# Adaptive-norm columns summed by VectorE alone, from weights laid out by output column

## The chip, the core and the metric

One core of a Trainium2 chip runs the program. Time is device microseconds of one execution, the median of three runs. TensorE (PE in the profile) multiplies, VectorE (DVE), ScalarE (ACT) and GpSimd (POOL) work on whole tiles, and SyncE (SP) issues the transfers (DMA).

## The reference, cut to what matters

One layer of a hybrid encoder on 1024 tokens of width 1024: an attention branch that selects 256 keys for each query, a state-space (SSD) branch, a merge, and a SwiGLU feed-forward part. Everything is float32. The part that the change touches is the modulation at the top, one vector of six times 1024 numbers:

```python
mod = (jax.nn.silu(c) @ ada_w + ada_b)[:, None, :]
shift_m, scale_m, gate_m, shift_f, scale_f, gate_f = jnp.split(mod, 6, axis=-1)
h = rmsnorm(x, pre_norm_mix) * (1.0 + scale_m) + shift_m
...                                            # both branches work on h
x = x + gate_m * rmsnorm(mix, post_norm_mix)
h2 = rmsnorm(x, pre_norm_ffn) * (1.0 + scale_f) + shift_f
```

and the state-space branch's time steps:

```python
dt = jax.nn.softplus((dt_raw + dt_bias).astype(jnp.float32))
dA = (dt * A).reshape(...);  a_cum = jnp.cumsum(dA, axis=-1)
decay = jnp.exp(a_cum[..., -1:] - a_cum);  chunk_decay = jnp.exp(a_cum[..., -1])
```

## The kernel before, in words

Activations lie transposed: 128 channels on the partitions, tokens along the row in two halves of 512. A product in float32 is three matmuls of rounded parts (high by high, high by low, low by high). Weights of the large products come through `Stream` (`wraw`, then `whi` by ScalarE at L158 and `wlo` by GpSimd or VectorE at L159), two pieces of 4 x 128 x 128 ahead of PE.

`mod` has 48 columns of 128 channels. The first 16 (shift and scale of the mixer) are made by PE right at the start (`ada_mm`, `ada_end`). The other 32 aren't needed before the merge, late in the program, and are made by `ada_slow`, one column j at a time: two halves of the weights (`adaw`, 128 input channels on the partitions, 4 x 128 output channels in the row, 256 KB each) are loaded into two buffers, GpSimd multiplies each by silu(c) (`cs`, L329) and adds the two (L330), VectorE sums the remaining four pieces (L331, into `adas`), and `ada_col` sums over the partitions with one matmul against a column of ones (L297, `adap`, two records in the profile) and adds the bias on VectorE (L298, into `mod`).

These columns are issued in the attention stage. `attention` goes through 32 steps: 8 head pairs `hp`, four blocks of 256 queries `u` each, in the order 0, 2, 1, 3 (`U_ORDER`). A step makes the queries (`puq`, then `qh` on ScalarE and `ql` on VectorE at L821), the logits of two tiles of 128 queries and two heads (`plg`, L847), adds bias or mask and takes the running extreme on VectorE (L856, `lg` and `mx`), takes exponentials on ScalarE, and in the same step transposes the probabilities of the step before (`pt`, copied to `pc` by VectorE or ScalarE) and multiplies them with the values (`po`, L896). Blocks u = 2 and 3 have two `plg` banks to each tile and head and twelve `mx` pieces; u = 0 has four. Convolution work of the state-space branch is woven in (`fill`: `pw` on PE at L244, `cv` on VectorE at L1073, L1075 and L1090). PSUM places come from two rings: `bank`, five deep (`puq`, `plg`, `po`, `adap`, every other `pt`), and `bank_d`, three deep. At a step's end `beside()` calls `ada_next`, which starts column j and finishes the one started three steps before:

```python
    def ada_next():
        next(sums, None)
        j = next(slow, None)
        if late and (j is None or len(late) > 2):
            ada_col(*late.pop(0))
        if j is not None:
            late.append(ada_slow(j))
```

Ahead of attention stand the input projections (`FILL`: five groups of convolutions, 16 tiles of z, 8 of a gate), and beside them the indexer, whose `rel` pieces VectorE weights with `widx` and sums into `acc` (L654), and the search for the 256th largest score (`Ranked`). The state-space branch's `dt`, `acum`, `decay` and `cdec` are made in `dt_part` before the indexer and are used after attention, in `ssd_in` and `ssd_out`.

What sets the order: a scheduler places each engine's instructions by a simulated clock when the program is built, under the data's own dependences and those added by hand. In attention PE runs in the order written (`in_order`), the other engines don't. Every engine and SP's queue of transfers works through its own list in order and waits at its head.

Of the kernel before, what the change touches and what calls it, by code (L numbers as in the profile page):

```python
# [69 lines left out]
def build(tc, a, dbg=None, stop=99, slots=None):  # L70
# [223 lines left out]

    def ada_col(j, acc):
        p = bank("adap")
        T.matmul(p[:, 0:1], acc, onec, start=True, stop=True)  # L297
        V.tensor_tensor(mod[:, j:j + 1], p[:, 0:1], col("ada_b", j), op=OP.add)  # L298

    cs32 = sm.tile([P, 8, 32], F32, name="cs32", tag="r2", bufs=1)  # L300
# [14 lines left out]
    def ada_end(k, acc):  # L315
# [4 lines left out]
        V.scalar_tensor_tensor(amul[:, k:k + 1], mod[:, 8 + k:9 + k], 1.0, col("pre_mix", k), op0=OP.add, op1=OP.mult)  # L320

    def ada_slow(j):

        acc = sm.tile([P, P], F32, name="adas", bufs=4)
        ts = [wp.tile([P, 4, P], F32, name="adaw", tag="adaw", bufs=2) for h in range(2)]
        for h, t in enumerate(ts):
            tc.add_manual_dep(SP.dma_start(t, a["ada_w"][j - 16][:, 4 * h:4 * h + 4]).ins, ada_after[0], mybir.DependencyInfo(
                mybir.DependencyClass.NoSync, mybir.DependencyReason.DATA), reason="behind")
            behind(G.tensor_tensor(t, t, cs[:, 4 * h:4 * h + 4, None].to_broadcast([P, 4, P]), op=OP.mult))  # L329
        G.tensor_tensor(ts[0], ts[0], ts[1], op=OP.add)  # L330
        V.tensor_reduce(acc, ts[0].rearrange("p k m -> p m k"), axis=AX.X, op=OP.add)  # L331
        return j, acc

# [203 lines left out]

    widx = con.tile([P, NT, 16], F32, name="widx")
    dt = con.tile([P, NT, 32], F32, name="dt")
    tmp = [R("dt_tmp", (P, 4, NT, 32)) for _ in range(2)]  # L540
# [10 lines left out]
    def dt_part():  # L551
# [23 lines left out]
        T.matmul(ptot[:, 0:128], ones, dAv[:, :, 1, :], start=False, stop=True)  # L575
        acum = con.tile([P, NT, 32], F32, name="acum")
# [3 lines left out]
        decay = con.tile([P, NT, 32], F32, name="decay")  # L580
# [3 lines left out]
        cdec = con.tile([P, NCH, 32], F32, name="cdec")  # L584
        S.activation(cdec, tot, AF.Exp)
# [10 lines left out]
        dump("acum", acum)  # L596
        return acum, decay, cdec

    acum, decay, cdec = dt_part()


# [327 lines left out]
    def attention(steps, beside, fill, nf):  # L929

        ahead = biases(*steps[0])
        for n, s_ in enumerate(steps + [None]):
            nxt = iter(())
            if s_ is not None:
                hp, u = s_
                if u == U_ORDER[0]:
                    vt = vp.tile([P, NT, P], F32, name="vt", bufs=1)
                    SP.dma_start(vt, d_v[hp])
                    att["w"] = small_weights(a["w_uq"][hp]), vt
                uq, vt = att["w"]  # L940
                PR = {}
                nms, ahead = ahead, biases(*steps[n + 1]) if n + 1 < len(steps) else None
                nxt = att_scores(u, uq, nms, PR)
            prev = att.get("prev")
            out, turns = (att_out(*prev), 2 * prev[1] + 2) if prev else (iter(()), 0)
            order = [nxt]
            for i in range(4):
                order += [out] * (-(-(i + 1) * turns // 4) - order.count(out)) + [nxt]
            order.append(out)
            k = 0  # L950
            for i, g in enumerate(order):
                next(g, None)
                while k < nf[n] and k * len(order) < nf[n] * (i + 1):
                    next(fill, None)
                    k += 1
            if s_ is not None:
                att["prev"] = (hp, u, vt, PR)
            beside()

    slow, late = iter(range(16, 48)), []  # L960

    def ada_next():

        next(sums, None)
        j = next(slow, None)
        if late and (j is None or len(late) > 2):
            ada_col(*late.pop(0))
        if j is not None:
            late.append(ada_slow(j))

# [168 lines left out]
    V.tensor_scalar(halved, halved, 0.5, None, op0=OP.mult)  # L1139
# [1021 lines left out]
def arrays_of(inp):  # L2161
# [53 lines left out]
```

## Time and profile before

| | |
|---|---|
| median of 3 runs | 2335.45 us (2332.7 to 2337.65) |
| the profiled execution | 2334.56 us, span 2332.5 us |
| PE busy | 2298.1 us, 99% |
| VectorE, ScalarE, GpSimd busy | 71%, 52%, 42% |
| granted clock of TensorE | 0.996 |
| attention | from 675 to 1116 us of the span |
| the 32 columns (L327 to L331) | transfers from 405 us on, last reduction at 1092 us |
| their `adap` matmuls | 719 to 1116 us |

A row of a group of instructions reads: line, engine, operation, what is written from what, shapes, count | busy us, mean ns of one | idle us of the engine before them and what ended it. A row of a window reads: from and to, length, then the busy time (and the count) of PE, PE's weight loads, VectorE, ScalarE and GpSimd, the clock granted, the share of the DMA engines and GB/s.

### The profile page before, as it was taken

Reading aid. Unit: us, or ns where it says so; the run is one execution under the profiler, and the core shown is the slowest. Engines: PE = TensorE matmul, PEld = TensorE weight load, DVE = VectorE, ACT = ScalarE, POOL = GpSimd, SP = SyncE. Lnnn points to the kernel's source line nnn. Section 1 sums busy time; section 2 is a strip of 40 time slices with the busy share of each in tenths; the row PEclk is TensorE's granted clock in tenths of the full one; section 3 lists DMA queues with packets and bytes.
Section 4 is the critical chain, followed back from the end, with each engine's and each line's share of the span. In section 5 each row is a group of like instructions: output and inputs, shape, how many; then the busy total and the mean of one; then the engine's idle time right before and its main releaser. Section 6 shows DMA issues by size and latency. Waiting matters only on the chain. (4 is left out here: it accounts for less than half of the span.)

```text
span 2332.5 us, 35045 instructions
## 1 busy us (share of the span) xinstructions
PE 2298.1 (99%) x11736; PEld 1886.0 (81%) x11736; DVE 1646.2 (71%) x3185; ACT 1220.1 (52%) x2354; POOL 985.3 (42%) x787
## 2 busy tenths in 40 slices
PE   8999999999999999999999999999999999999997
PEld 5878888888888888888888888878788888888886
DVE  5466887599676777677667879675778776646685
ACT  4346666467635555555767766434555222235542
POOL 1435552522244656564345443100122554444556
PEclk9999999999999999999999999999999999999998
DMA  7137542622233444344689999674573454438664
GB/s 274 64 126 246 190 172 93 200 96 95 100 111 123 130 129 141 128 132 142 210 254 291 296 275 326 223 229 144 182 244 125 154 162 155 145 116 274 202 201 155
DMA packets 251715, 411.26 MB, mean 176 GB/s; under 512 B 25568, under 2 KB 93328, under 8 KB 251536
## 3 DMA queue, kind: packets, MB, share of 16 engines
q1 hardware_dynamic: 238288, 387.48, 50.5%
q10 hardware_dynamic: 13248, 21.56, 3.1%
q8 instruction: 92, 1.51, 0.3%
q14 instruction: 87, 0.71, 0.1%
HBM read 304.84 MB, written 107.24 MB: 177 GB/s over the span
## 5 line engine op out<-in xcount | busy, mean ns | idle before, releaser
L159 POOL TENSOR_TENSOR wlo<-wraw,whi 128x512 fp32r<-128x512 f32 x152 | 208.2, 1370 | 305.5 <-ACT whi L158 277.8
L1774 PE MATMUL p<-xh,wr 128*128 128x512 f32 x880 | 271.8, 389 | 0.0
L158 ACT ACTIVATE whi<-wraw 128x512 fp32r<-128x512 f32 x238 | 149.1, 628 | 207.9 <-issue 58.7
L1774 PEld LDWEIGHTS p<-xh,wr 128*128 128x128 f32 x880 | 165.2, 188 | 34.3
L1768 POOL TENSOR_TENSOR wr<-a,wr 128x512 fp32r<-128x512 f32 x82 | 114.7, 1407 | 133.8 <-ACT wr L1767 104.1
L1774 PE MATMUL p<-xl,wr 128*128 128x512 f32 x440 | 171.2, 389 | 0.0
L255 POOL TENSOR_TENSOR fwl<-fw,fwh 128x512 fp32r<-128x512 f32 (+1 forms) x78 | 107.0, 1384 | 105.1 <-ACT fwh L254 59.6
L273 POOL TENSOR_TENSOR r<-v,nhalf 128x4 f32<-128x4 f32 (+1 forms) x17 | 25.5, 1499 | 255.4 <-DVE v L271 255.4
L1767 ACT ACTIVATE wr<-a 128x512 fp32r<-128x512 f32 x107 | 66.6, 629 | 126.2 <-PE p L1774 88.2
L859 ACT ACTIVATE lg<-lg,mx 128x256 f32<-128x256 f32 (+7 forms) x128 | 99.1, 774 | 57.8 <-DVE mx L856 57.3
L654 DVE SCALAR_TENSOR_TENSOR acc<-rel,widx,acc 128x384 f32<-128x384 f32 (+2 forms) x90 | 102.1, 1157 | 16.2 <-ACT rel L649 16.1
L329 POOL TENSOR_TENSOR adaw<-adaw,cs 128x512 f32<-128x512 f32 x64 | 68.1, 1065 | 102.5 <-DMA adaw<-ada_w 85.0
L1774 PE MATMUL p<-h2h,wr 128*128 128x512 f32 x352 | 110.0, 390 | 0.0
L704 ACT ACTIVATE junk<-acc,cand__2216 128x1024 bf16<-128x1024 f32 (+2 forms) x96 | 86.3, 898 | 39.5 <-DVE cand__2216 L747 30.7
L649 ACT ACTIVATE rel<-prel 128x512 f32<-128x512 f32 (+3 forms) x160 | 76.9, 523 | 47.1 <-PE prel L648 46.3
L1774 PEld LDWEIGHTS p<-xl,wr 128*128 128x128 f32 x440 | 82.6, 188 | 17.2
L1698 PE MATMUL pos<-yh,wlo 128*128 128x512 f32 x224 | 87.9, 392 | 2.2 <-DVE wlo L159 2.1
L702 DVE TENSOR_SCALAR_CACHE_REDUCE junk<-acc,cand__2225 128x896 bf16<-128x896 f32 (+2 forms) x96 | 88.5, 922 | 1.5
L856 DVE CUSTOM_DVE_ANT_0 lg<-plg,nm 128x256 f32<-128x256 f32 (+1 forms) x128 | 51.5, 403 | 52.7 <-PE plg L847 52.0
L1768 POOL TENSOR_TENSOR wr<-s,wr 128x512 fp32r<-128x512 f32 x40 | 55.0, 1375 | 78.4 <-ACT wr L1767 70.8
L1698 PE MATMUL pos<-yh,whi 128*128 128x512 f32 x224 | 87.8, 392 | 0.0
L1698 PE MATMUL pos<-yw,whi 128*128 128x512 f32 x224 | 87.3, 390 | 0.0
(692 smaller groups left out, 7415.4 us busy)
## 6 DMA issues: line engine op xcount, KB each, us to landing
wraw<-w_in SPq DMA_DIRECT2D x129, 256.0 KB, 2.9
a<-w_ffn_in SPq DMA_DIRECT2D x122, 256.0 KB, 3.4
al<-d_a SPq DMA_DIRECT2D x88, 256.0 KB, 4.5
yl<-d_y SPq DMA_DIRECT2D x72, 256.0 KB, 4.9
adaw<-ada_w SPq DMA_DIRECT2D x64, 256.0 KB, 3.2
al<-d_ac SPq DMA_DIRECT2D x32, 512.0 KB, 5.6
d_a<-g SPq DMA_DIRECT2D x42, 256.0 KB, 2.4
ada<-ada_p SPq DMA_DIRECT2D x16, 512.0 KB, 7.9
```

What stands on the lines that cost most here:

```text
L158: self.hi = behind(S.activation(hi[:, :kt], raw[:, :kt], AF.Copy))
L159: self.lo = behind(self.eng[len(self.tiles) % len(self.eng)].tensor_tensor(lo[:, :kt], raw[:, :kt], f(hi[:, :kt]), op=OP.subtract))
L255: (lo_eng or V).tensor_tensor(lo, src, f(hi), op=OP.subtract)
L329: behind(G.tensor_tensor(t, t, cs[:, 4 * h:4 * h + 4, None].to_broadcast([P, 4, P]), op=OP.mult))
L649: S.activation(rel[:, 512 * b:512 * b + w_], pr[:, 0:w_], AF.Relu)
L654: V.scalar_tensor_tensor(acc[i][:, 0:n], rel[:, 0:n], ws, acc[i][:, 0:n], op0=OP.mult, op1=OP.add)
L702: V.tensor_scalar(jk, y, a_, 0.0, op0=op, op1=OP.add, accum_out=o)
L704: S.activation(jk, y, AF.Sign, scale=-1.0, bias=a_, accum_out=o)
L859: S.activation(lg[:, 0:n], lg[:, 0:n], AF.Exp, scale=-1.0, bias=m, accum_out=rr[:, 2 * t + hh:2 * t + hh + 1])
L1698: T.matmul(p, w[k // 4][wi][:, k % 4], YO[i][k][xi], start=start and k == 0 and n == 0, stop=k == SK - 1 and n == 2, skip_group_check=True)
L1768: parts_last[0] = parts_eng[0].tensor_tensor(w[:, 1], src, f(w[:, 0]), op=OP.subtract).ins.name
L1774: T.matmul(p, w[:, wi, i], X[x][i][xi], start=start and i == 0 and k == 0, stop=i == 3 and k == 2, skip_group_check=True)
```

## The change

The weights of the 32 later columns are laid out on the host by output column (`ada_t`: 128 output channels on the partitions, the 1024 inputs in the row), and silu(c) stands as a row of 1024 numbers in every partition. One VectorE instruction then multiplies half a row (512) by its part of silu(c) and sums it, starting from the bias or from the first half's sum: two instructions to a column, no GpSimd work, no matmul. The row of silu(c) takes the place in SBUF (`steady`) of `dt`, `acum`, `decay`, `cdec` and `widx`; the first four are stored to DRAM (`d_kept`) when made, and loaded back when the columns are done. The columns begin with attention's second step, up to three halves to a step, written after items 2, 5 and 8 of it and behind VectorE's last instruction written until then.

```diff
-    def ada_col(j, acc):
-        p = bank("adap")
-        T.matmul(p[:, 0:1], acc, onec, start=True, stop=True)
-        V.tensor_tensor(mod[:, j:j + 1], p[:, 0:1], col("ada_b", j), op=OP.add)
...
+    def steady():
+        return con.tile([P, 1024], F32, name="steady", tag="steady")
+    def ada_rows():
+        cb = steady()
+        SP.dma_start(cb, a["c_row"][None, :].to_broadcast([P, D]))
+        S.activation(cb, cb, AF.Silu)
+        return cb
     def ada_slow(j):
-        acc = sm.tile([P, P], F32, name="adas", bufs=4)
-        ts = [wp.tile([P, 4, P], F32, name="adaw", tag="adaw", bufs=2) for h in range(2)]
-        for h, t in enumerate(ts):
-            tc.add_manual_dep(SP.dma_start(t, a["ada_w"][j - 16][:, 4 * h:4 * h + 4]).ins, ada_after[0], ...)
-            behind(G.tensor_tensor(t, t, cs[:, 4 * h:4 * h + 4, None].to_broadcast([P, 4, P]), op=OP.mult))
-        G.tensor_tensor(ts[0], ts[0], ts[1], op=OP.add)
-        V.tensor_reduce(acc, ts[0].rearrange("p k m -> p m k"), axis=AX.X, op=OP.add)
-        return j, acc
+        at = col("ada_b", j)
+        for h in range(2):
+            t = wp.tile([P, 4, P], F32, name="adaw", tag="adaw", bufs=2).rearrange("p k m -> p (k m)")
+            tc.add_manual_dep(SP.dma_start(t, a["ada_t"][j - 16][:, 512 * h:512 * h + 512]).ins, rows[1], ...)
+            to = mod[:, j:j + 1] if h else sm.tile([P, 1], F32, name="adas", bufs=4)
+            last = next(i for i in reversed(nc.cur_bb.bb.instructions) if i.engine == mybir.EngineType.DVE)
+            tc.add_manual_dep(V.tensor_tensor_reduce(t, t, rows[0][:, 512 * h:512 * h + 512], op0=OP.mult, op1=OP.add,
+                                                     scale=1.0, scalar=at, accum_out=to).ins, last.name, ...)
+            at = to
+            yield
...
+    kept = steady()
+    dt, acum, decay, cdec = consts(kept)
+    widx = kept[:, 896:1024].rearrange("p (t h) -> p t h", t=NT)
...
+        SP.dma_start(d_kept, kept[:, 0:896])              # end of dt_part
...
             for i, g in enumerate(order):                 # attention, items of step n
                 next(g, None)
+                if n and i in (2, 5, 8):
+                    next(slow, None)
...
-    slow, late = iter(range(16, 48)), []
+    rows = []
+    slow = (x for j in range(16, 48) for x in ada_slow(j))
     def ada_next():
         next(sums, None)
-        j = next(slow, None)
-        ...
...
+            if t == 12:                                   # FILL, the thirteenth tile of z
+                rows.append(ada_rows())
...
+    rows.append(W.issue)                                  # end of FILL
...
+    for _ in slow:                                        # after attention
+        pass
+    kept = steady()
+    SP.dma_start(kept[:, 0:896], d_kept)
+    dt, acum, decay, cdec = consts(kept)
```

How the change moves instructions, at three places. First PE at the end of an attention step, where the old column's matmul stood between the products with the values and the next step's queries; the names are those of the section above. Before:

```order
L892 MATMUL po<-ident,r_6823 128x128 x2
L896 MATMUL po<-pc,vt 64x256 x14
L896 MATMUL po<-pc,vt 64x128 x2
L297 MATMUL adap<-ones,adas 128x1
L234 MATMUL puq<-qnh,uh 128x256
```

After (lines are those of the changed kernel, 1 to 13 higher here):

```order
L905 MATMUL po<-ident,r_6645 128x128 x2
L909 MATMUL po<-pc,vt 64x256 x6
L909 MATMUL po<-pc,vt 64x128 x2
L235 MATMUL puq<-qnh,uh 128x256
L235 MATMUL puq<-qnl,uh 128x256
```

`puq` now follows `po` directly, and `puq` takes the place in the ring of five that `adap` took.

Second VectorE in the middle of a step u = 2 with convolution work, from the first tile's and head's last `mx` on. Before:

```order
L856 ISA lg,mx<-plg,mk,mx 128x256
L856 ISA mx 128x1
L856 ISA lg,mx<-plg,nm 128x256
L856 ISA mx 128x1
L1073 SCALAR_TENSOR_TENSOR cv<-pw,vec,cv 128x509
L1075 SCALAR_TENSOR_TENSOR cv<-ends,vec,cv 128x3
L883 COPY pc<-pt 128x2x128
L856 ISA lg,mx<-plg,mk,mx 128x128
```

After:

```order
L869 ISA lg,mx<-plg,mk,mx 128x256
L869 ISA mx 128x1
L338 ISA adaw,mod<-adaw,steady,adas 128x512
L338 ISA mod 128x1
L869 ISA lg,mx<-plg,nm 128x256
L869 ISA mx 128x1
L1084 SCALAR_TENSOR_TENSOR cv<-pw,vec,cv 128x509
L1086 SCALAR_TENSOR_TENSOR cv<-ends,vec,cv 128x3
L896 COPY pc<-pt 128x2x128
L869 ISA lg,mx<-plg,nm 128x256
```

One new piece (L338, with the read of its sum) now stands between the first three `mx` of the step and the rest.

Third VectorE at the end of the same step, from its last `mx` on. Before:

```order
L856 ISA lg,mx<-plg,mk,mx 128x256
L856 ISA mx 128x1
L856 ISA lg,mx<-plg,mk,mx 128x256
L856 ISA mx 128x1
L298 TENSOR_TENSOR mod<-adap,vec 128x1
L331 TENSOR_REDUCE adas<-adaw 128x128
L900 TENSOR_TENSOR rb<-po,rb 128x256
L856 ISA lg,mx<-plg,mk,mx 128x256
L856 ISA mx 128x1
L821 SCALAR_TENSOR_TENSOR ql<-puq,qh 128x512
```

After:

```order
L869 ISA lg,mx<-plg,mk,mx 128x256
L869 ISA mx 128x1
L338 ISA adaw,adas<-adaw,steady,vec 128x512
L338 ISA adas 128x1
L869 ISA lg,mx<-plg,mk,mx 128x256
L869 ISA mx 128x1
L913 TENSOR_TENSOR rb<-po,rb 128x256
L869 ISA lg,mx<-plg,mk,mx 128x256
L869 ISA mx 128x1
L834 SCALAR_TENSOR_TENSOR ql<-puq,qh 128x512
```

`mod` and `adas`, which stood behind the step's `mx` and ahead of `rb` and the next step's `ql`, are gone from there; the second new piece stands ahead of the last two `mx`.

In SP's queue the transfer of the row of c stands where the first two of the old columns' transfers stood, at the end of the indexer, with weight loads ahead of it and behind it; it waits for the last use of `widx`. The columns' own transfers are now spread over attention's steps 2 to 25.

More of the change, by code (lines that the diff above doesn't have):

```diff
@@ L223, in build @@
     d_skew = dr.tile([16, P, 384], F32, name="d_skew")
+    d_kept = dr.tile([P, 896], F32, name="d_kept")
     d_v = dr.tile([8, P, 8, P], F32, name="d_v")
@@ L320, in ada_end @@
         V.scalar_tensor_tensor(amul[:, k:k + 1], mod[:, 8 + k:9 + k], 1.0, col("pre_mix", k), op0=OP.add, op1=OP.mult)
+    def steady():
[5 more added lines that the diff above has]
+        return cb
     def ada_slow(j):
-        acc = sm.tile([P, P], F32, name="adas", bufs=4)
-        ts = [wp.tile([P, 4, P], F32, name="adaw", tag="adaw", bufs=2) for h in range(2)]
-        for h, t in enumerate(ts):
-            tc.add_manual_dep(SP.dma_start(t, a["ada_w"][j - 16][:, 4 * h:4 * h + 4]).ins, ada_after[0], mybir.DependencyInfo(
+        at = col("ada_b", j)
+        for h in range(2):
+            t = wp.tile([P, 4, P], F32, name="adaw", tag="adaw", bufs=2).rearrange("p k m -> p (k m)")
+            tc.add_manual_dep(SP.dma_start(t, a["ada_t"][j - 16][:, 512 * h:512 * h + 512]).ins, rows[1], mybir.DependencyInfo(
                 mybir.DependencyClass.NoSync, mybir.DependencyReason.DATA), reason="behind")
-            behind(G.tensor_tensor(t, t, cs[:, 4 * h:4 * h + 4, None].to_broadcast([P, 4, P]), op=OP.mult))
-        G.tensor_tensor(ts[0], ts[0], ts[1], op=OP.add)
-        V.tensor_reduce(acc, ts[0].rearrange("p k m -> p m k"), axis=AX.X, op=OP.add)
-        return j, acc
+            to = mod[:, j:j + 1] if h else sm.tile([P, 1], F32, name="adas", bufs=4)
+            last = next(i for i in reversed(nc.cur_bb.bb.instructions) if i.engine == mybir.EngineType.DVE)
+            tc.add_manual_dep(V.tensor_tensor_reduce(t, t, rows[0][:, 512 * h:512 * h + 512], op0=OP.mult, op1=OP.add,
+                                                     scale=1.0, scalar=at, accum_out=to).ins, last.name, mybir.DependencyInfo(
+                mybir.DependencyClass.NoSync, mybir.DependencyReason.DATA), reason="behind")
+            at = to
+            yield
     AHEAD = 2
@@ L536, in build, with consts @@
         dump("kn", kn[0:64], (slice(None), half(b)))
-    widx = con.tile([P, NT, 16], F32, name="widx")
-    dt = con.tile([P, NT, 32], F32, name="dt")
+    def consts(kept):
+        return (kept[:, 0:256].rearrange("p (t h) -> p t h", t=NT), kept[:, 256:512].rearrange("p (t h) -> p t h", t=NT),
+                kept[:, 512:768].rearrange("p (t h) -> p t h", t=NT), kept[:, 768:896].rearrange("p (c h) -> p c h", c=NCH))
+    kept = steady()
+    dt, acum, decay, cdec = consts(kept)
+    widx = kept[:, 896:1024].rearrange("p (t h) -> p t h", t=NT)
     tmp = [R("dt_tmp", (P, 4, NT, 32)) for _ in range(2)]
@@ L575, in dt_part @@
         T.matmul(ptot[:, 0:128], ones, dAv[:, :, 1, :], start=False, stop=True)
-        acum = con.tile([P, NT, 32], F32, name="acum")
         V.tensor_copy(acum.rearrange("p t h -> p (t h)"), pc[:, 0:256])
@@ L579, in dt_part @@
         V.tensor_copy(tot.rearrange("p c h -> p (c h)"), ptot[:, 0:128])
-        decay = con.tile([P, NT, 32], F32, name="decay")
         V.tensor_tensor(decay.rearrange("p (c t) h -> p c t h", t=2), tot[:, :, None, :].to_broadcast([P, NCH, 2, 32]),
@@ L583, in dt_part @@
         S.activation(decay, decay, AF.Exp)
-        cdec = con.tile([P, NCH, 32], F32, name="cdec")
         S.activation(cdec, tot, AF.Exp)
@@ L596, in dt_part @@
         dump("acum", acum)
-        return acum, decay, cdec
-    acum, decay, cdec = dt_part()
+        SP.dma_start(d_kept, kept[:, 0:896])
+    dt_part()
     bt = R("btmp", (P, 1024))
@@ L958, in attention @@
             beside()
-    slow, late = iter(range(16, 48)), []
+    rows = []
+    slow = (x for j in range(16, 48) for x in ada_slow(j))
     def ada_next():
         next(sums, None)
-        j = next(slow, None)
[L966 to L969, printed above, removed]
     def wide(c):
@@ L2166, in arrays_of @@
     ada = g["ada_w"]
-    out["ada_w"] = pack(ada[:, 2048:])
+    out["ada_t"] = np.ascontiguousarray(ada[:, 2048:].T).reshape(32, P, D)
+    out["c_row"] = np.ascontiguousarray(g["c"][0])
     out["ada_p"] = np.ascontiguousarray(ada[:, 0:2048].reshape(2, 4, P, 2, 8, P).transpose(4, 0, 2, 1, 3, 5)).reshape(8, 2, P, 4, 256)
```

## The prediction

> **What bounds the kernel now.** I read the page's busy times first, then the stages of the span, then what TensorE (PE) waits for, then single steps of the attention stage.
>
> ```profile
> span 2332.5 us, 35045 instructions
> PE 2298.1 (99%) x11736; PEld 1886.0 (81%) x11736; DVE 1646.2 (71%) x3185; ACT 1220.1 (52%) x2354; POOL 985.3 (42%) x787
> ```
>
> PE is idle for 34 us in all. Work taken off another engine is worth nothing unless PE was waiting for it; work taken off PE is worth its full time. The windows by stage (PE, PEld, DVE, ACT, POOL busy, granted clock, DMA) put the change's work in place: projections and top-k search to 675, attention to 1116, the part of attention in which the new reductions stand to 1005.
>
> ```profile
> 405.00:675.00 270.00, 269.61 (x1206) 222.88 (x1205) 206.53 (x608) 157.00 (x311) 91.66 (x72) 1.00 0.36 119
> 675.00:1005.00 330.00, 325.32 (x2133) 271.78 (x2132) 230.29 (x701) 183.94 (x381) 192.75 (x182) 1.00 0.41 131
> 1005.00:1116.00 111.00, 109.98 (x739) 90.56 (x738) 75.08 (x231) 64.69 (x134) 56.99 (x54) 1.00 0.47 149
> ```
>
> Attention leaves PE idle for 5.7 us of 441. The waits of PE there (total us, times, longest):
>
> ```profile
> PE adap L297 <- DVE mx L856: 2.7, 4, 0.8
> PE puq L234 <- DVE mx L856: 1.2, 4, 0.3
> PE plg L847 <- DVE ql L821: 1.0, 2, 0.5
> ```
>
> All three are waits for VectorE (DVE), and two begin at the matmul that the change removes.
>
> **The matmuls removed.** Each of 32 columns ends with one `adap` matmul (two records) between a step's `po` and the next step's `puq`. The timeline of PE:
>
> ```profile
> 717.42 1.73 PE L896 MATMUL po<-pc,vt 128*64 128x256 f32 x16
> 719.08 0.38 PE L297 MATMUL adap<-ones,adas 128*128 128x1 f32 x2
> 719.33 0.36 PE L234 MATMUL puq<-qnh,uh 128*128 128x256 f32 x1
> ```
>
> From the start of `adap` to the start of `puq` PE gives 719.33 - 719.08 = 0.25 us; nothing runs beside it. Gain: 32 x 0.25 = **8.0 us**. The rule that would speak against it is the Trainium skill's, "TensorE: Matmul & The Clock Gate", section "Wait — 56ns, not 53.3ns?": start to start never falls below about 25 ns however few columns stream. An estimate by that floor alone is 64 x 0.025 = 1.6 us; the trace has five times that per matmul, and the trace is what I use.
>
> **The waits at the step's end.** One step of four (u = 2) runs VectorE nearly full. One head pair's steps u = 0, 2, 1, 3, same columns as above:
>
> ```profile
> 722.20:736.10 13.90, 13.90 (x107) 11.74 (x106) 6.03 (x19) 7.31 (x17) 10.74 (x10) 1.00 0.64 207
> 736.10:749.10 13.00, 11.93 (x73) 9.97 (x72) 11.82 (x37) 6.35 (x13) 8.69 (x9) 1.00 0.50 163
> 749.10:763.20 14.10, 14.10 (x95) 11.55 (x95) 9.52 (x29) 8.82 (x19) 7.04 (x9) 1.00 0.31 90
> 763.20:779.10 15.90, 15.90 (x100) 13.24 (x98) 12.55 (x37) 8.91 (x16) 9.30 (x9) 1.00 0.29 89
> ```
>
> DVE has 7.9, 1.2, 4.6 and 3.3 us to spare. The end of the full one, on both engines:
>
> ```profile
> 743.72 1.76 DVE L1090 SCALAR_TENSOR_TENSOR cv<-th,cv 128x512 f32<-128x512 f32 x1
> 745.40 0.47 DVE L856 CUSTOM_DVE_ANT_0 lg<-plg,mk,mx 128x256 f32<-128x256 f32 x1
> 746.97 0.14 DVE L298 TENSOR_TENSOR mod<-adap,vec 128x1 f32<-128x1 f32 x1
> 747.03 1.08 DVE L331 TENSOR_REDUCE adas<-adaw 128x128 f32<-128x512 f32 x1
> ...
> 746.03 0.35 PE L297 MATMUL adap<-ones,adas 128*128 128x1 f32 x2 [0.76 <-DVE mx L856]
> 746.69 0.39 PE L234 MATMUL puq<-qnh,uh 128*128 128x256 f32 x1 [0.30 <-DVE mx L856]
> ```
>
> `adap` waits for its PSUM bank, one of five, which the `mx` at 745.40 frees; `puq` waits for the next bank. Without `adap`, `puq` takes the bank that `adap` took, so 0.7 us of wait moves to it and does not go; the second wait (row 1.2 us, four times) goes, since the bank behind it is next asked for only after `ql`. Gain: **1.2 us**.
>
> The wait for `ql` has the old reduction ahead of it in DVE's queue:
>
> ```profile
> 776.83 0.14 DVE L298 TENSOR_TENSOR mod<-adap,vec 128x1 f32<-128x1 f32 x1
> 776.90 1.08 DVE L331 TENSOR_REDUCE adas<-adaw 128x128 f32<-128x512 f32 x1
> 779.08 0.68 DVE L821 SCALAR_TENSOR_TENSOR ql<-puq,qh 128x512 fp32r<-128x512 f32 x1
> ```
>
> These 1.2 us leave that place, and PE waited 0.5 us there: gain **1.0 us** for the two times.
>
> **What VectorE gets.** 64 multiply-and-sum instructions of 128x512 (`adaw` by the row, sum into `adas` or `mod`), 11 to each head pair, so over the first 24 of 32 steps. The trace has the same operation on PSUM in `lg`, with the read of its accumulator, and an addition with both inputs in SBUF (`cv<-th,cv`):
>
> ```profile
> L856 DVE CUSTOM_DVE_ANT_0 lg<-plg,mk,mx 128x512 f32<-128x512 f32 x14 | 10.5, 749 | 1.8 <-DVE mx L856 0.5
> L856 DVE DVE_READ_ACCUMULATOR2_ANT mx<- 128x1 f32 x260 | 21.2, 81 | 0.0
> L1090 DVE SCALAR_TENSOR_TENSOR cv<-th,cv 128x512 f32<-128x512 f32 x22 | 21.3, 966 | 0.7
> ```
> ```profile
> L1090 DVE SCALAR_TENSOR_TENSOR cv<-th,cv x24: 685/708/1760, 688.1 to 1110.2; 128x512 f32<-128x512 f32 x24
> L331 DVE TENSOR_REDUCE adas<-adaw x32: 1058/1080/1107, 413.7 to 1092.4; 128x128 f32<-128x512 f32 x32
> ```
>
> Lower bound 0.75 + 0.08 = 0.83 us. Two SBUF inputs stretch `cv<-th,cv` from 0.69 to as much as 1.76, by 0.28 in the mean, while the old reduction, with one input, keeps within 0.05. So the upper bound is 1.9 us a piece. GpSimd (POOL) is busy 250 of 441 us of attention now and loses these (27 columns fall into attention):
>
> ```profile
> L329 POOL TENSOR_TENSOR adaw<-adaw,cs 128x512 f32<-128x512 f32 x53 | 55.2, 1041 | 84.4 <-DMA adaw<-ada_w 76.8 <-DVE cv L1073 3.0 <-DVE mx L856 2.7
> L330 POOL TENSOR_TENSOR adaw<-adaw 128x512 f32<-128x512 f32 x27 | 35.5, 1315 | 1.3
> ```
>
> That leaves 159 of 441, six tenths of before, so I take 0.28 x 0.6 = 0.16 of stretch: 0.99 us each, nearest to the unstretched row. The Trainium skill ("SBUF — State Buffer", section "Who interferes with whom") says that a VectorE instruction with two SBUF inputs and a GpSimd instruction that reads SBUF shut each other out for the whole instruction, and that `tensor_reduce` never contends. The two rows with their spread agree. Without that rule the pieces would cost 64 x 0.83 = 53 us, with it 63 us.
>
> In sum DVE gets 63 us and loses 32 x (1.08 + 0.14) = 39; it has 100 us idle in 675 to 1005, so it doesn't become the bound on average. It matters where it stands:
> - u = 2 with convolution work (3 steps): one piece now stands ahead of the `mx` that frees the bank; +0.99, less some 0.4 of the stretch seen in the 1.76 us row. **+0.6 each, 1.8.** Bounds 0 and 1.9.
> - u = 2 without it (3 steps, no wait now): 0.3 each, between nothing and a piece: **0.9**.
> - u = 0 (6 steps): three pieces close together; 7.9 us idle cover the work, not always the transfers. 0.2 each, between 0 and one landing (3.2): **1.2**.
> - u = 1 and 3 (12 steps): idle 4.6 and 3.3 against 3 x 0.99 less 1.22 = 1.8 more work; 0.1 each: **1.2**.
>
> POOL's loss of 91 us there is worth nothing to PE: no wait of PE in attention names it.
>
> **The transfers.** Still 64 of 256 KB, in two buffers, now freed by DVE instead of POOL:
>
> ```profile
> L327 SPq DMA_DIRECT2D adaw<-ada_w x64: 327/332/818, 405.1 to 1079.9; - x64
> DMA to landing us min/median/max: 2.5/3.2/5.8
> ```
> ```profile
> POOL adaw L329 <- DMA adaw<-ada_w: 85.0, 42, 4.3
> ```
>
> A buffer comes back 0.33 + 3.2 = 3.5 us after its piece ends; two pieces on is 2 x 14 / 2.75 = 10 us on the mean, but 4 to 5 us in u = 0. Queued behind a waiting piece on DVE are the `mx` that free PE's banks.
>
> **The row and the constants.** The broadcast of c waits for the last read of `widx` (the indexer's last accumulation), and SiLU for the broadcast, nearest to this one:
>
> ```profile
> 408.14 3.22 DVE L654 SCALAR_TENSOR_TENSOR acc<-rel,widx,acc 128x896 f32<-128x896 f32 x2 [0.68 <-ACT rel L649]
> 417.16 0.60 ACT L981 ACTIVATE g<-pw 128x512 f32<-128x512 f32 x1 [2.26 <-PE pw L234]
> 421.06 0.63 ACT L158 ACTIVATE whi<-wraw 128x512 fp32r<-128x512 f32 x1 [1.99 <-PE pw L234]
> ```
> ```profile
> al<-d_ac SPq DMA_DIRECT2D x32, 512.0 KB, 5.6
> ```
>
> 411.4 + 5.6 = 417.0, SiLU on 1024 columns some 1.1 us, done at 418.2; ScalarE's next `whi` runs at 421.06 anyway. SP waits to 411.4 with weight loads behind it, 3 us on loads that are two pieces ahead. I take 0, between 0 and 3. The store is one issue early; the reload lands around 1010 us, and the constants are first read after it:
>
> ```profile
> L1212 POOL TENSOR_TENSOR Xd<-X,decay x24: 1042/1100/2029, 1120.5 to 1392.3; 128x512 f32<-128x512 f32 x24
> ```
>
> That is 100 us of cover: 0.
>
> **Sum.** -8.0 - 1.2 - 1.0 + 1.8 + 0.9 + 1.2 + 1.2 = -5.1. The profiled execution took 2334.56 (its span and 2.1 around it): 2329.5. The median of before is 2335.45, 0.9 above it, within the spread of its three runs; I leave the forecast at **2329.5**.
>
> **Rivals.**
> - *VectorE gives it back* (no change). If each u = 2 step loses 1.5 instead of 0.6 or 0.3 and each u = 3 step 0.4: 9.0 + 2.4 in place of 2.7 and 0.6, so +8.1: 2337.6 at the far end, and 2334 half-way. For it: 1.2 us to spare. Against: in u = 3 PE didn't wait for `mx` at the step's end.
> - *Late transfers hold VectorE* (slower). POOL took 85 us of waits for `ada_w` off the path; in DVE's queue they would stand ahead of `mx`. A mean wait of w per piece costs a u = 2 step about 1.5 w and a u = 3 step 3 w less the 1.5 us that it still has idle: 9 w + (18 w - 9). From w = 0.5 us the gain is gone; at 0.8, 2334.56 - 5.1 + 12.6 = 2342; at POOL's whole 85 / 64 = 1.3, 2356. Against: 10 us of mean spacing for a transfer of 3.5.
> - *No new waits* (more gain): POOL's absence frees DVE, none of the 5.1 us of new waits comes, and the 2.7 us of `adap` goes: 2334.56 - 8.0 - 1.2 - 1.0 - 2.7 = 2321.7.
> - *It doesn't do what it says*: the scheduler's new order up to 675 loses PE more than it had idle (0.4 us in the last 270); 1 to 5 us, inside the range.
>
> **Chances.** Forecast (2325 to 2332.5) 0.52; given back (2332.5 to 2339) 0.24; late transfers (above 2339) 0.13; no new waits 0.11. A measurement here tells about 0.2%, 4.7 us: faster means below 2330.8. Four fifths of the forecast and all of the last make 0.51 faster; most of the second and the rest of the first 0.35 same; 0.14 slower. Range 2321.5 to 2339, which leaves out the late transfers and little below.
>
> **What would show it.** No `adap` records after 63 us and `puq` right behind `po`; the pieces at 0.9 to 1.1 us on DVE; `puq` waiting for `mx` about 1.4 us in three steps; DVE's wait for `ada_t` under 10 us in all; attention ending 5 us sooner. Wrong, if PE's waits in attention exceed 10 us, or if stages ahead of 675 move by over 2 us.

## The result, and the profile after

The changed kernel took 2320.87 us (median of 6 runs, 2318.16 to 2322.02), before 2334.64 (6 runs beside it): ratio 0.9937, 95% interval 0.9924 to 0.995, so 13.8 us or 0.6% less. The forecast was 2329.5. The profiled execution took 2321.74.

The head of its page, to be held against the two lines of before:

```profile
span 2319.8 us, 34896 instructions
PE 2293.4 (99%) x11672; PEld 1880.2 (81%) x11672; DVE 1650.2 (71%) x3249; ACT 1216.7 (52%) x2355; POOL 883.8 (38%) x691
```

GpSimd (POOL) has 101.5 us less to do, VectorE (DVE) 4 us more, PE 4.7 less. Where the span got shorter is shown by windows cut at the first `puq`, the first `pcb` (end of attention) and the first `pfo` (last stage); columns as before. Before:

```profile
673.00:1116.40 443.40, 437.70 (x2887) 364.65 (x2885) 305.54 (x933) 250.37 (x517) 251.15 (x238) 1.00 0.43 136
2098.80:2332.50 233.70, 219.92 (x1035) 183.79 (x1033) 153.22 (x204) 101.25 (x184) 126.67 (x98) 0.97 0.65 208
```

After:

```profile
674.00:1107.40 433.40, 431.97 (x2824) 356.63 (x2823) 314.59 (x1003) 244.28 (x516) 165.35 (x159) 1.00 0.45 145
2090.00:2319.80 229.80, 217.80 (x1035) 182.84 (x1033) 149.56 (x202) 100.76 (x182) 125.96 (x98) 0.98 0.66 210
```

Up to attention the span changed by +1.0 us, in attention by -10.0 (-10.1 from matmul to matmul), from there to the last stage by +0.2, in the last stage by -3.9. Attention lost 5.7 us of PE's busy time and 4.3 us of its idle time. What PE (TensorE) still waits for there (us in all, times, longest):

```profile
PE plg L860 <- ACT qh L833: 0.5, 2, 0.3
PE pt L893 <- ACT lg L872: 0.2, 1, 0.2
```

The waits for `mx` and `ql` are gone, and none came for them. The convolution's addition, the new pieces, and VectorE's wait for their loads:

```profile
L1101 DVE SCALAR_TENSOR_TENSOR cv<-th,cv x24: 677/684/1325, 689.9 to 1101.8; 128x512 f32<-128x512 f32 x24
L338 DVE CUSTOM_DVE_ANT_0 adaw<-adaw,steady,vec x32: 736/748/1772, 688.2 to 991.9; 128x512 f32<-128x512 f32 x32
L338 DVE CUSTOM_DVE_ANT_0 adaw<-adaw,steady,adas x32: 739/744/1090, 692.4 to 996.0; 128x512 f32<-128x512 f32 x32
```
```profile
DVE adaw L338 <- DMA adaw<-ada_t: 8.7, 7, 2.7
```

`cv<-th,cv` has a mean of 0.73 us where it had 0.94. A piece, as the text calls one multiply-and-sum instruction of the change, takes 0.87 in the mean, and 0.08 more to read its sum. The full step (u = 2) of the same head pair as before, its windows and its end on both engines:

```profile
736.80:749.50 12.70, 12.49 (x74) 10.12 (x74) 11.26 (x39) 6.62 (x14) 4.27 (x4) 1.00 0.36 127
```
```profile
745.33 0.68 DVE L1101 SCALAR_TENSOR_TENSOR cv<-th,cv 128x512 f32<-128x512 f32 x1
745.93 0.47 DVE L869 CUSTOM_DVE_ANT_0 lg<-plg,mk,mx 128x256 f32<-128x256 f32 x1
...
745.92 0.87 PE L909 MATMUL po<-pc,vt 128*64 128x256 f32 x8
746.72 0.38 PE L235 MATMUL puq<-qnh,uh 128*128 128x256 f32 x1
```

The addition that took 1.76 us at this place takes 0.68; the `mx` behind it comes in time, and `puq` starts right behind `po`. VectorE is busy 11.26 us in this step, with two pieces in it (at 742.18 and 747.09), where it was busy 11.82 with the old reduction and addition, and GpSimd 4.27 in place of 8.69.

### The profile page after: what moved, and what is told of

Its sections match the earlier page's. It is cut to its first block, busy times and chain, and to the rows that moved or that the text cites. A ratio compares the mean times of both kernels' runs of the same rounds, so it can differ in the third digit from the quotient of the medians.

```text
span 2319.8 us, 34896 instructions
## 1 busy us (share of the span) xinstructions
PE 2293.4 (99%) x11672; PEld 1880.2 (81%) x11672; DVE 1650.2 (71%) x3249; ACT 1216.7 (52%) x2355; POOL 883.8 (38%) x691
## 5 line engine op out<-in xcount | busy, mean ns | idle before, releaser
L667 DVE SCALAR_TENSOR_TENSOR acc<-rel,steady,acc 128x384 f32<-128x384 f32 (+2 forms) x90 | 103.1, 1175 | 13.6 <-ACT rel L662 13.5
L159 DVE TENSOR_TENSOR wlo<-wraw,whi 128x512 fp32r<-128x512 f32 x86 | 60.2, 701 | 34.1 <-ACT whi L158 33.9
L893 PE MATMUL pt<-ident,lg 128*128 128x128 f32 x576 | 82.8, 273 | 0.2 <-ACT lg L872 0.2
```

The source lines that it names most:

```text
L159: self.lo = behind(self.eng[len(self.tiles) % len(self.eng)].tensor_tensor(lo[:, :kt], raw[:, :kt], f(hi[:, :kt]), op=OP.subtract))
L667: V.scalar_tensor_tensor(acc[i][:, 0:n], rel[:, 0:n], ws, acc[i][:, 0:n], op0=OP.mult, op1=OP.add)
L893: T.transpose(ptv[:, hh, t, :], PR[hh, t][:, j * P:(j + 1) * P], ident)
```

## The experiments

Attention is measured in each profile from the first `puq` to the first `pcb`. "PE idle", the mean of `cv<-th,cv` (column `cv`), the mean piece and GpSimd's busy time are of that stretch. The ratio is to before, run on the same chip. Each run has one profile: before and its repeat differ by 3.4 us of attention, the changed kernel and its repeat by 1.7, so a difference of that size between two rows tells nothing by itself.

| run | attention | PE idle | `cv` | piece | GpSimd | ratio, 95% interval |
|---|---|---|---|---|---|---|
| before | 443.5 | 5.7 | 0.94 | | 251 | |
| before_same | 446.9 | 7.3 | 0.95 | | 251 | 1.0008, 0.9995 to 1.0021 |
| before_no_pool | 436.5 | 0.1 | 0.73 | | 161 | 0.9967, 0.9955 to 0.9979 |
| before_no_matmul_held | 435.1 | 4.0 | 0.70 | | 249 | 0.9973, 0.9962 to 0.9984 |
| before_ring_three | 441.4 | 4.3 | 0.95 | | 253 | 0.9998, 0.9987 to 1.0008 |
| before_dram | 443.4 | 5.3 | 1.00 | | 251 | 1.0001, 0.9991 to 1.0011 |
| after | 433.3 | 1.4 | 0.73 | 0.87 | 165 | 0.9937, 0.9924 to 0.995 |
| after_same | 431.6 | 0.9 | 0.79 | 0.90 | 165 | 0.9929, 0.9917 to 0.9941 |
| adap_back_five | 438.7 | 0.9 | 0.76 | 0.88 | 167 | 0.9958, 0.9946 to 0.997 |
| adap_back_three | 438.0 | 0.7 | 0.77 | 0.88 | 167 | 0.9963, 0.9952 to 0.9975 |
| after_pool_tile | 447.8 | 13.1 | 1.10 | 0.99 | 295 | 1.0006, 0.9998 to 1.0015 |
| after_pool_write | 436.6 | 4.1 | 0.70 | 0.82 | 263 | 0.994, 0.9927 to 0.9953 |
| after_no_pieces | 429.3 | 0.5 | 0.70 | | 163 | 0.9915, 0.9901 to 0.9928 |
| after_not_full | 429.6 | 0.4 | 0.77 | 0.91 | 165 | 0.9925, 0.9912 to 0.9937 |
| after_two | 431.0 | 1.8 | 0.77 | 0.83 | 167 | 0.996, 0.9948 to 0.9972 |

**The matmul, put back.** To the changed kernel, at the end of each attention step (the line that makes the empty list `adap_n` is left out here):

```diff
+        if len(adap_n) < 32:
+            adap_n.append(1)
+            T.matmul(bank("adap")[:, 0:1], ones, onec, start=True, stop=True)
```

> The changed kernel with one 128x1 matmul per attention step put back at the step's end (32 in all), in the ring of five banks where the old one stood; its result is read by nobody and everything else is as changed. Matmul time alone: 32 x 0.25 = 8.0 us back, about 2329 us, the profile showing 0.25 us start to start per matmul and no new wait. Ring place: the old one also took a bank that `mx` frees late; if that place made the old waits, the 2.7 us before the matmul and the 1.2 us before `puq` come back as well, 8.0 + 3.9: about 2333. If GpSimd's load made these waits, they stay away here (GpSimd has nothing back) and PE's idle time in attention stays under 1 us.

The second with `bank_d` in place of `bank`:

> As the run before, with the 32 matmuls in the ring of three banks, so that `puq` keeps the bank it has in the changed kernel. Matmul time alone: 2329 us again, within 1 us of the ring of five. Ring place: 8.0 us back and no wait, 2329, and 3 to 4 us less than the ring of five. So the two runs together separate the matmul's own time (both) from the place that it takes in the ring (their difference).

Measured: 2325.53 and 2326.84 us, 4.7 to 7.4 over the two medians of the changed kernel (2320.87, 2319.45). From the start of `adap` to the start of the next matmul the 32 take 8.3 and 7.7 us. No wait returned in either ring. So the matmul's own time is shown, 0.24 to 0.26 us each from start to start, of which 0.15 to 0.23 reach the medians; its place in the ring made no wait in these two runs, in which VectorE was in time.

**The matmul, taken away alone.** From the kernel before:

```diff
-        T.matmul(p[:, 0:1], acc, onec, start=True, stop=True)
-        V.tensor_tensor(mod[:, j:j + 1], p[:, 0:1], col("ada_b", j), op=OP.add)
+        V.tensor_tensor(mod[:, j:j + 1], acc[:, 0:1], col("ada_b", j), op=OP.add)
```

> The kernel before without the matmul `adap`; VectorE adds the bias to the first column of the reduction's output, so the sum over partitions is left out. GpSimd's and VectorE's work stays. By the prediction's steps: 8.0 for the matmuls and 1.2 for the second wait go, 2.7 us of wait moves to `puq` and stays: time 2325.5, attention about 435.5, `puq` waiting 0.7 us for `mx` four times. If the wait went with the matmul and its bank: attention 432.5 to 433, as in the changed kernel, time 2323. By the runs with the matmul put back, which cost 5 to 6.5 us and not 8: attention 437 and time 2328.

A miss: 2375.56 us. Nothing held the columns any more, and the scheduler pulled all 32 ahead of attention. The row of GpSimd's products shows it:

```profile
L327 POOL TENSOR_TENSOR adaw<-adaw,cs x64: 1038/1041/2016, 411.1 to 672.3; 128x512 f32<-128x512 f32 x64
```

They came ahead of GpSimd's other work there: PE waited 33 us for ScalarE's `g` between 400 and 725, in before 0.4, and attention began at 724 in place of 673. The same edit, with the addition tied in the order to the matmul ahead of it:

> The kernel before without the matmul `adap` (the sum over partitions is left out), with VectorE's addition held in its place in the order, so that PE's order is that of before less 32 matmuls and GpSimd's products stay in attention. By the prediction's steps: matmuls 8.0 and second wait 1.2 go, 2.7 us of wait stays with `puq`: attention 434.2, time 2325.5. If all 3.9 us of waits at the step's end go with the matmul: attention 431.5, time 2322.7. If VectorE's lateness under GpSimd's load sets the step's end whatever PE does: waits of 5 us or more, attention 435 to 437, time 2326 to 2328.

Measured: 2330.14 us (ratio 0.9973), slower than each of the three expectations; attention 435.1 in the profile, which is of the fastest of nine executions. No wait of `puq` is left; PE waits elsewhere:

```profile
PE plg L847 <- DVE mx L856: 1.7, 2, 1.0
PE pt L880 <- ACT lg L859: 1.7, 5, 0.4
PE plg L847 <- ACT qh L820: 0.3, 1, 0.3
```

So the 2.7 us did not move to `puq`, as the prediction had it, but 3.7 us of waits of other kinds stand there. In this run `cv` kept to 0.70 although GpSimd did all its products: the same load met other instructions. The bias addition, `mod<-adas,vec`, now has both inputs in SBUF, where before's, `mod<-adap,vec`, read one from PSUM. It took 0.41 us in the mean and 1.26 at most, for 0.15 and 0.16, so the run has some 8 us more on VectorE than the prediction's steps allow for.

**The ring alone.** In the kernel before, `bank("adap")` became `bank_d("adap")`.

> The kernel before with `adap` in the ring of three banks in place of the ring of five; nothing else. The `mx` that frees the bank of five comes as late as before, so the next one to ask for it, `puq`, waits in place of `adap` and the matmul's 0.25 us hides inside that wait: 1.2 us less, and four waits of `puq` of some 0.4 to 0.7 us; time 2333.5. If the ring's place made the waits: 3.9 us less, attention 439.5, time 2331. If it is of no account: 2334 to 2335.

Measured: no difference in time. Attention was 2.1 us shorter in the profile, no more than two profiles of before differ by; `puq` waited 0.2 to 0.4 us four times and `pt` for `lg` 0.55 four times. The waits changed places, and PE idle fell by 1.4 us.

**GpSimd's work, taken away alone.** From the kernel before:

```diff
-            behind(G.tensor_tensor(t, t, cs[...].to_broadcast([P, 4, P]), op=OP.mult))
-        G.tensor_tensor(ts[0], ts[0], ts[1], op=OP.add)
```

> The kernel before without GpSimd's two products and one sum per column; VectorE's reduction reads the first loaded half as it came, so 32 columns of the modulation are left out of the result. The matmul `adap`, VectorE's reduction, its addition and all loads stay. GpSimd's relief as the cause of the missing waits: PE's waits for `mx` and `ql` in attention (4.9 us) go almost whole, attention falls from 443 to about 438.5, `cv` from a mean of 0.95 to 0.73 us, time about 2330. If the waits come from VectorE's own queue (the reduction and the addition that stand in it) and not from GpSimd: attention 443 within 1 us, time 2334 to 2335.

Measured: 2327.31 us (ratio 0.9967). Attention, with all 32 matmuls and reductions still in it, and the `cv` row:

```profile
672.20:1108.70 436.50, 436.37 (x2888) 364.39 (x2886) 293.69 (x934) 250.05 (x517) 161.23 (x158) 1.00 0.43 138
```
```profile
L1088 DVE SCALAR_TENSOR_TENSOR cv<-th,cv x24: 676/691/1476, 687.3 to 1102.4; 128x512 f32<-128x512 f32 x24
```

PE's idle time fell from 5.7 to 0.1 us. VectorE's busy time fell by 11.9 us (305.54 to 293.69) with the same instructions on it; PE, VectorE and ScalarE have the same order of instructions in both traces, and no wait of VectorE in before's attention names GpSimd. The whole fall lies in two groups, both with two inputs in SBUF: `cv<-th,cv` lost 5.0 us in all, and the small `cv<-ends,vec,cv` 7.9 (sums of durations, which overlap a little); no other group of VectorE moved by more than 0.13. The small ones, before and in this run:

```profile
L1075 DVE SCALAR_TENSOR_TENSOR cv<-ends,vec,cv x36: 201/213/1299, 699.6 to 1108.6; 128x1 f32<-128x1 f32 x12, 128x2 f32<-128x2 f32 x12, 128x3 f32<-128x3 f32 x12
L1073 DVE SCALAR_TENSOR_TENSOR cv<-ends,vec,cv x36: 202/211/924, 699.0 to 1100.8; 128x1 f32<-128x1 f32 x12, 128x2 f32<-128x2 f32 x12, 128x3 f32<-128x3 f32 x12
```

In the medians the run is 7.3 us faster than before (4.9 to 10.5), beside 7.0 in the two profiles. This shows the largest part of attention that the prediction left out.

**GpSimd's work, put back.** First as two products and a sum per column on a scratch tile, from the row of weights alone:

> The changed kernel with GpSimd's old work put back on a scratch tile: per column two 128x512 products and one sum, both inputs in SBUF, from the first 512 and second 512 columns of a tile of weights; nobody reads the result, though a tile of weights now comes free only when GpSimd is done too. GpSimd's relief as the reason that the forecast new waits did not come: `cv` and the pieces on VectorE stretch again (`cv` from a mean of 0.73 to 0.9 or more, pieces from 0.79 to 0.9 or more), waits of PE for `mx` and `ql` return, 4 to 9 us: 2325 to 2330. If the relief is of no account: under 1 us, about 2321 to 2322, PE's idle time in attention under 1 us.

A miss: 2367.27 us. Nothing tied these instructions to a column, all 96 ran ahead of attention, PE waited 33 us for ScalarE's `g` there, and attention began at 721; attention itself took 432.1. Then tied to the loaded tile, behind each piece:

```diff
+            G.tensor_tensor(busy, t, rows[0][:, 512 * h:512 * h + 512], op=OP.mult)
+            if h:
+                G.tensor_tensor(busy, busy, rows[0][:, 0:512], op=OP.add)
```

> The changed kernel with GpSimd's old work put back where it can't run early: behind each piece a 128x512 product of the loaded tile with the row of weights on a scratch tile, and behind every second one a sum, results read by nobody. The two buffers of loaded weights come free only when GpSimd is done, about as before. The orders of PE and ScalarE are as in the changed kernel. GpSimd's relief as the cause: `cv` back to a mean of 0.9 or more, pieces to 0.9 or more, waits of PE for `mx` and `ql` of 3 to 8 us, attention from 432.5 to 436 to 440, time 2324 to 2328. If the relief is of no account: attention within 1 us of 432.5, time 2319 to 2321. If VectorE's pieces now wait for later loads, that shows as waits of the pieces for DMA over the 8.7 us of the changed kernel.

Measured: 2336.34 us (ratio 1.0006), the whole gain gone. PE's waits in attention, and `cv`:

```profile
PE plg L864 <- DVE ql L838: 3.1, 6, 0.6
PE pt L897 <- ACT lg L876: 2.2, 6, 0.8
PE plg L864 <- DVE pc L900: 2.2, 3, 0.7
PE puq L235 <- DVE mx L873: 2.1, 3, 0.8
PE plg L864 <- ACT qh L837: 2.0, 3, 0.7
PE plg L864 <- DVE mx L873: 1.4, 3, 0.9
```
```profile
L1105 DVE SCALAR_TENSOR_TENSOR cv<-th,cv x24: 671/774/1784, 685.8 to 1112.1; 128x512 f32<-128x512 f32 x24
L339 DVE CUSTOM_DVE_ANT_0 adaw<-adaw,steady,vec x32: 740/1088/1759, 684.1 to 1002.0; 128x512 f32<-128x512 f32 x32
```

This run overdoes it: its products take 1.3 us where those of before took 1.04, so GpSimd is busy 295 us and not 251. It also brings buffers back later. The next run parts the two: fills of the loaded tile in place of products (`G.memset(t, 0.0)`, two behind a column's first piece, four behind its second).

> As the run with GpSimd's work behind each piece, but GpSimd only writes: two 128x512 fills of the loaded tile behind a column's first piece and four behind its second, in place of products and a sum. Each buffer of loaded weights still comes free only when GpSimd is done; no fill reads SBUF. No row shows the duration of a fill; it may be under the 1.3 us of a product. If GpSimd costs VectorE time because its instructions read SBUF beside VectorE's two inputs: `cv` back at a mean of 0.73 to 0.8 us, attention 431.5 to 434, time 2319 to 2322. If it is GpSimd's queue or the late return of the buffers: attention 438 to 448, pieces waiting 10 to 16 us for loads, time 2326 to 2336.

Measured: 2323.4 us (ratio 0.994), between the two expectations. The fills with VectorE's wait for the loads (us in all, times; 8.7 in 7 in the changed kernel), `cv`, and PE's longest wait:

```profile
L343 POOL MEMSET adaw<- x192: 517/525/533, 690.8 to 1004.6; 128x512 f32 x192
...
  DVE adaw L338: 13.8, 10
```
```profile
L1103 DVE SCALAR_TENSOR_TENSOR cv<-th,cv x24: 680/688/898, 686.2 to 1101.3; 128x512 f32<-128x512 f32 x24
```
```profile
PE plg L862 <- DVE ql L836: 1.9, 2, 1.2
```

GpSimd is busy 263 us, more than before, yet `cv` never exceeds 0.90. So both theories may hold a part. GpSimd's queue and the later return of the buffers cost 3.3 to 5.0 us of attention in the profile (436.6 against 433.3 and 431.6); the time does not show it, as the ratio of 0.994 lies within the interval of the changed kernel. The rest of after_pool_tile's loss, 447.8 - 436.6 = 11.2 us, and 12.9 us between the medians, came with GpSimd reading SBUF. PE's and ScalarE's orders are the same in both runs. Little of the loss can be later buffers, since VectorE's wait for loads was 16.4 us there against 13.8 here, beside one of 5.0 here that is put down to GpSimd's `r`.

**The pieces.** In the changed kernel each piece became a 128x1 addition:

```diff
-            V.tensor_tensor_reduce(t, t, rows[0][...], op0=OP.mult, op1=OP.add, scale=1.0, scalar=at, accum_out=to)
+            V.tensor_tensor(to, t[:, 0:1], at, op=OP.add)
```

> The changed kernel with each piece on VectorE cut to a 128x1 addition that reads one column of the loaded tile, so the modulation's later columns are left out; loads and order of PE stay. The prediction charged the pieces 5.1 us of new waits: attention then 428, time 2315. If VectorE hides them, since GpSimd no longer stretches its other work: attention 431 to 433, within 1 us of the changed kernel's PE waits (1.4 and 0.9 us idle in its two profiles), time 2319 to 2321.

Then all pieces kept, none in the steps u = 2:

```diff
-                if n and i in (2, 5, 8):
+                if n and i in (2, 5, 8) and not (s_ and s_[1] == 2):
```

> The changed kernel without pieces in the steps u = 2, whose VectorE work is nearly full; three each in the other steps instead, up to the end of attention. The prediction charged u = 2 with 2.7 of its 5.1 us: attention 430 to 431.5, time 2318 to 2319. If the full steps cost nothing by now, since GpSimd no longer stretches them: attention 431.5 to 433.5, time 2319 to 2321.

Attention in the two runs:

```profile
672.50:1101.90 429.40, 428.87 (x2824) 357.19 (x2822) 275.47 (x939) 248.22 (x516) 162.62 (x159) 1.00 0.45 146
```
```profile
672.80:1102.30 429.50, 429.06 (x2823) 356.94 (x2821) 315.66 (x1003) 242.87 (x516) 164.51 (x159) 1.00 0.46 147
```

after_no_pieces took 2316.67 us, between its two expectations. Against 433.3 and 431.6 the pieces cost 2.3 to 4.0 us of attention in the profiles, and kept out of the full steps they cost nothing, with 40 us more on VectorE. PE's order is the same in all of them; VectorE's other instructions partly stand in another order, which the runs do not part from the pieces themselves. after_not_full is 2318.22 us; the intervals of both runs overlap that of the changed kernel, so the times do not show them to be faster, only attention in the profiles.

Two pieces per step through all 32 steps (`i in (2, 6)`):

> The changed kernel with two pieces per attention step in all 32 steps, in place of three in the first 22. The pieces cost 2 to 4 us of PE's time in the changed kernel. If they cost it where three stand close to a full step: attention 430 to 431.5, time 2317.5 to 2319. If each piece costs the same wherever it stands: attention 431.5 to 433.5, time 2319 to 2321. If the last steps, which hold no piece now, have less room: above that.

Attention came out as expected (431.0), but the time is 2325.79 us and not 2317.5 to 2319. Now the last piece ends at 1102, the row of SiLU(c) gives its place back only then, and the kept constants are reloaded at 1105.5 (996.8 in the changed kernel):

```profile
L1167 SPq DMA_DIRECT2D steady<-d_kept x1: 332/332/332, 1105.5 to 1105.5; - x1
```
```profile
PE pyd L1257 <- DVE al L1212: 4.0, 1, 4.0
```

The cover that the prediction named for this reload, 100 us, is used up, and PE waits 4.0 us in the next stage.

**What lies outside attention.** The changed kernel and the kernel before again, unchanged, and before with the changed kernel's DRAM buffer and input and two short transfers into that buffer:

> The changed kernel again, unchanged, for a second profile. In the profiles the stretch from the first `pfo` matmul to the end took 233.7 us before and 229.9 us after, with the same order of instructions on every engine. If that is chance from one execution to the next, the second profile differs by several us there; if it belongs to the changed kernel, 229.9 within 1 us again. Time 2321 either way, attention ending some 10 us ahead of the kernel before when counted from its own start.

> The kernel before, unchanged, for a second profile. The stretch from the first `pfo` matmul to the end took 233.7 us in its first profile, 229.5 to 230.5 in the changed kernel and most of its variants, 230.5 to 233.1 in variants of before. If chance sets it, this one may lie anywhere from 229.5 to 233.7; if the kernel does, at 233.7 within 0.5. Attention 443.4 within 2 us, PE idle there 5 to 6 us.

> The kernel before with the buffer `d_kept` in DRAM and the input `c_row` that the changed kernel has, and two short transfers into that buffer; no engine's work is changed. In every profile with the layout of before the first `al` of the last stage becomes ready so late that ScalarE's first `ah` starts 3.2 to 3.7 us ahead of the first `pfo`; in every one with the layout of the changed kernel 4.75 us ahead. If the layout of DRAM makes this: `ah` at 4.75 here, the last stage 229.5 to 230.5 us in place of 231.8 to 233.7, time 2331 to 2333. If it does not: `ah` at 3.2 to 3.7, last stage 231.8 to 233.7, time 2334 to 2336.

Before's second profile had attention at 446.9 and PE idle at 7.3, above what was expected. The last stage took 229.9 in the changed kernel's second profile too. Before's second took 231.8 in place of 233.7, with the same wait of PE for `sqm` near its end; the difference is the granted clock behind that wait (third number from the end of each row: 0.85 and 0.81, against 1.00 and 1.00):

```profile
2288.80:2293.80 5.00, 3.75 (x17) 3.02 (x17) 1.59 (x3) 2.11 (x5) 5.00 (x5) 0.85 0.54 147
2293.80:2298.80 5.00, 5.00 (x20) 4.04 (x19) 1.01 (x1) 2.31 (x4) 4.58 (x5) 0.81 0.28 88
```
```profile
2294.70:2299.70 5.00, 3.87 (x21) 3.38 (x22) 1.60 (x3) 1.90 (x5) 5.00 (x5) 1.00 0.50 147
2299.70:2304.70 5.00, 5.00 (x26) 4.18 (x25) 1.43 (x2) 2.19 (x4) 4.69 (x5) 1.00 0.26 80
```

Of the other 2 us, 1.2 are that wait for `sqm`: PE waits for it 2.0 us in both profiles of before and 0.8 and 0.7 in the two of the changed kernel. A difference that is seen ahead of it is ScalarE's first conversion of `al`, here in before and in before_dram:

```profile
2095.60 0.63 ACT L1950 ACTIVATE ah<-al 128x512 fp32r<-128x512 f32 x1 [1.42 <-DMA al<-d_a]
```
```profile
2093.38 0.62 ACT L1953 ACTIVATE ah<-al 128x512 fp32r<-128x512 f32 x1
```

That is 3.2 and 4.75 us ahead of the first `pfo`. In six profiles with the layout of before it lies between 3.2 and 3.7, in all with `d_kept` and `c_row` at 4.75. So the added buffer and input, or the two transfers, make the load come earlier, with no instruction of the last stage changed; before_dram waited 0.8 us for `sqm`, and its last stage took 230.7. That the load's lead makes that wait is not shown: before_no_pool has a lead of 3.65, waited 1.1 and took 230.5. The time of before_dram did not follow: 1.0001, with 2.1 us of gain as the far end of the interval. What the earlier load is worth in the median stays open.

## Why the prediction was wrong, by its steps

The forecast for attention was -5.1; the profile gave -10.1. Taken apart by before_no_pool, after_no_pieces and the changed kernel: 443.5 to 436.5 without GpSimd's products (-7.0), to 429.3 without matmul and reduction (-7.2), to 433.3 with the pieces (+4.0; 431.6 in the second profile, as before has 446.9 in its second). The forecast's terms for the three were -3.4, -8.0 and +6.3, so 3.6 of the 5.0 us between forecast and profile are GpSimd's, 2.3 the pieces', and the matmuls take 0.8 off again.

- **The matmuls: right.** -8.0 was forecast. Put back, they take 8.3 and 7.7 from start to start, and 4.7 to 7.4 in the medians; between before_no_pool and after_no_pieces lie 7.2. The 25 ns that the Trainium skill names as the least distance between starts ("TensorE: Matmul & The Clock Gate", section "Wait — 56ns, not 53.3ns?") would have made 1.6: the runs bear out the trace's 0.25 us per matmul, not that estimate.
- **"POOL's loss of 91 us there is worth nothing to PE": this step failed.** It rested on the row that no wait of PE names GpSimd. None does, but the waits for `mx` and `ql` stood behind VectorE instructions that GpSimd had stretched. Taking only GpSimd's work away removes all of PE's 5.7 us, the wait for `ql` with the old reduction still ahead of it included, and 7.0 of attention. For all that the sum had 1.2 + 1.0 for waits, laid to the matmul and the reduction, and 0.4 of relief in each of three full steps: 3.4.
- **The mechanism was in the text, but on one side of the account only.** The rule of the Trainium skill ("SBUF — State Buffer", section "Who interferes with whom"), that a VectorE instruction with two SBUF inputs and a GpSimd instruction that reads SBUF shut each other out, was used to price the pieces. By the same rule the removed products free `cv`: 1.76 us at 743.72 became 0.68. That the rule spares instructions that only write is borne out too: fills leave `cv` at 0.70, products bring it to 1.10. The price of a piece, 0.99 with the read of its sum, was nearly right: it measured 0.95 and 0.98 so counted, and 1.07 with GpSimd's load put back.
- **The wait that "moves" to `puq`: wrong.** Without the matmul `puq` did not wait in before_no_matmul_held, nor in the changed kernel; 1.4 us had been forecast for three steps. With GpSimd's load still there, 3.7 us of waits stood elsewhere; with it gone too, PE idled 0.5 us (after_no_pieces).
- **New waits of 5.1 us: half right.** u = 2 was charged 2.7; keeping the pieces out of it is worth 2.1 to 3.8 of attention in the profiles. u = 0, 1 and 3 were charged 2.4 and cost nothing: after_not_full has pieces only there, and PE idles 0.4 us.
- **The transfers, the row and the constants: right.** VectorE waited 8.7 us for loads, under 10, and nothing was seen to wait for SiLU(c) or the reload. The first reader of the constants is not `Xd`, as the prediction read it, but ScalarE's `M` (1111.0 in before, 1102.6 in the changed kernel); the reload, issued at 996.8, landed 5.3 us later, so the cover of 100 us holds. after_two shows that it can be used up.
- **Stages ahead of 675: right**, +1.0. The last stage was not thought of at all: 3.9 us in the profiles, of which 1.9 is the clock of one execution. How much of it is in the medians, the runs do not show.
- **The chances:** by its own fractions a faster result comes to 0.53, not 0.51.

The rival that came nearest was "no new waits", at 2321.7. It named the mechanism, GpSimd's absence, but its number agrees in part by chance: it put 12.9 us into attention, where the profile has 10.0, and none into the last stage.

## What to carry to other kernels

A wait names the engine that came last, not the one that made it late: where an instruction of that engine spreads upward (0.69 to 1.76 us here), ask what it met, and count the removal of that as a gain on the path. In these profiles, work added to a busy engine cost time only where a step had no room; keep it out of the full steps, and check what its end releases.

## What the hardware showed that was not expected

- GpSimd's fills of 128x512 (0.525 us each, 192 of them) did not stretch `cv<-th,cv` or the pieces: `cv` kept to 0.70 and a piece to 0.82, beside 0.73 and 0.87 without the fills. With products and sums of the same size `cv` rose to 1.10, and by up to 1.1 us in one instruction.
- One 128x1 instruction took 0.88 us in the changed kernel (0.21 is its group's median there) beside two additions of GpSimd. Of the 12.9 us by which VectorE's instructions got shorter in before_no_pool, 7.9 were those of this group:

```profile
739.54 2.29 POOL L819 TENSOR_TENSOR nm<-nb,mk 128x512 f32<-128x512 f32 x2
...
739.84 0.88 DVE L1086 SCALAR_TENSOR_TENSOR cv<-ends,vec,cv 128x1 f32<-128x1 f32 x1
```

- A gap of 1.3 to 1.8 us between two starts of PE near the end was followed, 1 to 2 us on, by 3.4 us at a granted clock of about half (0.50 or 0.51; 2292.3 to 2295.7 in before) in three of five profiles (before, before_ring_three, before_no_matmul_held) and by no such fall in the other two (before_same, before_no_matmul); in before it cost 1.9 us in one execution and nothing in the next. What decides it, the runs do not show. The Trainium skill ("TensorE: Matmul & The Clock Gate", section "Part 1: The HAM clock gate (the "warmup" mystery)") names a free-running window of activity, so that the same kernel meets it at another phase each time. That fits, though the page has the clock fall only after an idle window of about 3.4 us, and here the clock fell behind gaps of 1.3 to 1.8 us.
